# Dropping the step between load and first use where a tile was loaded ahead, and giving attention one more before its scores

## The chip, the cores and the metric

The kernel runs on one core of a Trainium2 chip, in one launch. The metric is device time in microseconds: the median of three runs. Names of engines: TensorE (PE in the profile, its weight loads PEld), VectorE (DVE), ScalarE (ACT), GpSimd (POOL), SyncE (SP, which issues the DMAs).

## The reference

One layer of an encoder, y = x + W_out @ concat[SSD, windowed attention, memory attention](RMSNorm(x)), in float32. It is applied to 1024 and to 256 tokens with shared weights: ten tiles of 128 tokens, with D_MODEL = 2048. Cut to what matters:

```python
proj = rms_norm(x, norm_g) @ w_in
xbc, z_ssd, dt_raw, q, k, v, z_att, mq, z_mem = split_cols(proj, IN_SIZES)
# SSD: conv + silu on xbc, a chunked scan forwards and backwards, gate, norm
o_ssd = rms_norm((y_f + y_b + d_skip * xs) * silu(z_ssd), ssd_norm_g)
# attention: 8 query heads and 2 key heads of 64, |t - s| <= 128, ALiBi, one sink logit a head
q, k = rms_norm(q, q_norm_g), rms_norm(k, k_norm_g)
o_att = window_attention(q, k, v, sink) * silu(z_att)
# memory attention: 4 heads of 128 over 256 memory rows
mk, mv = split_cols(rms_norm(mem, mem_norm_g) @ w_mem_kv, (MEM_WIDTH, MEM_WIDTH))
mq, mk = rms_norm(mq, mq_norm_g), rms_norm(mk, mk_norm_g)
o_mem = softmax(mq @ mk.T * 128 ** -0.5) @ mv * silu(z_mem)
y = x + concat([o_ssd, o_att, o_mem]) @ w_out
```

## The kernel before, in words

**The large products.** Rows of x (and later of the mixed outputs) stand on chip as a high and a low part (`xH`, `xL`, float32r); weights stream from DRAM in tiles `wraw` and are split into `wh` on ScalarE (L206) and `wl` on VectorE (L207). Each product is three matmuls: high by high, high by low, low by high. `block_tok` makes a block of 512 columns for five token tiles (L258 to L260, 15 matmuls of 128x512 for each of 16 steps k); `block_feat` makes 256 features by 640 tokens (L293 to L295); `block_pair` makes pairs of half blocks from sums of weights (L1268 to L1270). The rings: three or four buffers for `wraw`, four each for `wh` and `wl` (`RB`, `WB`), five PSUM banks `acc` for the blocks and three PSUM buffers `mix` (`psum(...)`) for everything else.

**The small work beside them.** Key preparation (`k_prep`), windowed attention (`attn`), memory attention (`mem_attn`) and the SSD scan (`dt_prep`, `ssd_up`, `ssd_down`) are Python generators, one for each tile of 128 tokens. They stand in two queues, `lanes`: lane 0 holds keys, attention and memory attention, lane 1 the SSD. While a block is built, `pump` resumes the generators so many times for each k as `RATES` says for that block (some 2 each for every k of `block_tok`, half of it for `block_feat`). What a generator issues from one `yield` to the next is a step. Steps thus set where its instructions stand among the block's. A scheduler then orders each engine's instructions by priority and by its estimate of when they can start, so neighbours in program order may change places; the weight splits have a raised priority. Each engine works through its list in order.

**Loading ahead.** `attn`, `mem_attn` and `k_prep` call `fetch_next` shortly before they end. It looks at the next entry of lane 0 and, if it is one of these three kinds, issues the DMA of its rows (`k_fetch`, `q_fetch`, `mq_fetch`, L485 to L498) into the pool `wa` of five buffers, and keeps the buffer in `fetched`. The next generator begins with `taken(...)`, which gives that buffer, or issues the load itself if there is none. Before the change every generator then yields once, loaded ahead or not, before the first instruction that reads the rows: a Square on ScalarE (L517 in `k_prep`, L632 in `attn`, L749 in `mem_attn`), or, in `mem_attn` for tiles 0 to 4, whose rows are stored the other way round, four transposes on TensorE (`pmq`, L744).

**Attention.** After the Square come the sums and the power on GpSimd, the scaling of q, and in two halves the split copies `qh`, four transposes into PSUM `pq` (L653) and the copy to `qT` (L655). One step later `scores(0)` begins: two matmuls a head into `psc` (L671, L672), a fused minimum on VectorE (L673), the exponential on ScalarE (L677), then transposes `ppt` (L693) with copies `pT` on ScalarE (L694), and the products with the values `po` (L703).

The order in which the work is queued in lane 0 is: `mem_values`, `k_prep` 0 to 4, `attn` 0 to 3, `mem_attn` 0 to 4, `k_prep` 5 to 9, `attn` 4, `attn` 5 to 9; later `mem_attn` 5 to 7, `mem_swap`, `mem_values`, `mem_attn` 8 and 9.

Of the kernel before, what the change touches and what calls it, by code (L numbers as in the profile page):

```python
# [44 lines left out]
def hymba_encoder_kernel(  # L45
# [37 lines left out]
    def psum(name):  # L83
        return mix.tile([P, 512], F32, tag="mix", name=name)
# [37 lines left out]
    def rsqrt(dst, src, scale, n):  # L122
        G.tensor_scalar(out=dst, in0=src, scalar1=scale, scalar2=EPS, op0=ALU.mult, op1=ALU.add)
        G.tensor_tensor(out=dst, in0=dst, in1=mhalf[:, :n], op=ALU.pow)

    def hv(ap, n=8):
        return ap.rearrange("p (h d) -> p h d", h=n)

    def hb(ap, n, d):
        return ap.unsqueeze(2).broadcast_to([P, n, d])  # L130
# [284 lines left out]
    def w2(name):  # L415
        return mp.tile([P, 512], F32, tag="wa", name=name, bufs=WA)
# [64 lines left out]
    fetched = {}  # L481
# [21 lines left out]
    def taken(name, t):  # L503
        return fetched.pop((name, t)) if (name, t) in fetched else fetch[name](t)

    def fetch_next():

        name = lanes[0][1][0] if len(lanes[0]) > 1 else ("", 0)
        if name[0] in fetch:
            fetched[name] = fetch[name[0]](name[1])  # L510

    def k_prep(t):
        r = taken("k_prep", t)
        yield
        ss = sm.tile([P, 2], F32, tag="s2", name="kss", bufs=4)
        sq = w2("ksq")[:, :P]
        A.activation(sq, r, AF.Square)  # L517
        V.reduce_sum(out=ss, in_=hv(sq, 2), axis=AX.X)
        rr = sm.tile([P, 2], F32, tag="s2", name="krr", bufs=4)
        rsqrt(rr, ss, 1.0 / 64, 2)  # L520
        yield
        r3 = hv(r, 2)
        V.tensor_mul(r3, r3, hb(rr, 2, 64))
        V.tensor_mul(r3, r3, gq.unsqueeze(1).broadcast_to([P, 2, 64]))

        kh = mp.tile([P, 4, 2, 64], F32R, tag="wa", name="kh", bufs=WA)
        for d in range(2):
            A.activation(kh[:, 0:2, d, :], r3, AF.Copy)
        for d in range(2):
            V.tensor_sub(kh[:, 2:4, d, :], r3, kh[:, 0:2, 0, :].bitcast(F32))  # L530
        yield
        yield
        ps = psum("pk")
        kf = kh.rearrange("p a b d -> p (a b d)")
        for a in range(4):
            T.transpose(ps[:, a * P:(a + 1) * P].bitcast(F32R), kf[:, a * P:(a + 1) * P], identr)
        sl = t if t < 5 else t - 3
        c = slice(sl * P, (sl + 1) * P)
        V.tensor_copy(kT[:, :, c], hv(ps[:, :256], 2))
        A.activation(kL[:, :, c], hv(ps[:, 256:], 2), AF.Copy)  # L540
        fetch_next()
        yield
# [77 lines left out]
    def attn(t):  # L620
# [5 lines left out]
        s0 = k0 if t < 4 else k0 - 3  # L626
        grp, ti = divmod(t, 5)
        tc_ = slice(ti * P, (ti + 1) * P)
        q = taken("attn", t)
        yield  # L630
        sq = w2("sq")
        A.activation(sq, q, AF.Square)  # L632
        ss = sm.tile([P, 8], F32, tag="s8", name="qss", bufs=4)
# [22 lines left out]
            qT.append(o)  # L656
        z = w2("za")
        S.dma_start(hv(z, 4), zT_d[0][grp][:, :, tc_])
        yield
        ns8 = nsink.rearrange("p (v r) -> p r v", v=2)  # L660
        state_ = {}
# [72 lines left out]
    def mem_attn(t):  # L734
        grp, ti = divmod(t, 5)
        tc_ = slice(ti * P, (ti + 1) * P)
        qr = taken("mem_attn", t)
        q = qr.bitcast(F32)
        yield

        def turned():
            ps = psum("pmq")
            for h in range(4):
                T.transpose(ps[:, h * P:(h + 1) * P].bitcast(F32R), qr[:, h * P:(h + 1) * P], identr)  # L744
            return ps

        tok_ = turned() if grp == 0 else q
        sq = w2("sq")
        A.activation(sq, tok_, AF.Square)  # L749
        ss = sm.tile([P, 4], F32, tag="s4", name="mss", bufs=4)  # L750
        V.reduce_sum(out=ss, in_=hv(sq, 4), axis=AX.X)
        r = sm.tile([P, 4], F32, tag="s4", name="mr", bufs=4)
        rsqrt(r, ss, 1.0 / P, 4)
        yield
        feat_ = q if grp == 0 else turned()
        qh = mp.tile([P, 512], F32R, tag="qT", name="mqh", bufs=2)
        A.activation(qh, feat_, AF.Copy)
        ql = mp.tile([P, 512], F32R, tag="qT", name="mql", bufs=2)
        V.tensor_sub(ql, feat_, qh.bitcast(F32))
        z = w2("zm")  # L760
        S.dma_start(hv(z, 4), zT_d[1][grp][:, :, tc_])
        yield
        yield
        st_ = {}

        def scores(hp):
            ps = psum("pms")
            for j in range(2):
                h = 2 * hp + j
                c = slice(h * P, (h + 1) * P)  # L770
                o = ps[:, j * 256:(j + 1) * 256]
                T.matmul(o, qh[:, c], mkH[:, h, :], start=True, stop=False)
                T.matmul(o, qh[:, c], mkL[:, h, :], start=False, stop=False)
                T.matmul(o, ql[:, c], mkH[:, h, :], start=False, stop=True)
            m = sm.tile([P, 2], F32, tag="m2", name="mm", bufs=10)
            V.reduce_max(out=m, in_=hv(ps, 2), axis=AX.X)
            V.scalar_tensor_tensor(out=m, in0=m, scalar=-1.0, in1=r[:, 2 * hp:2 * hp + 2], op0=ALU.mult, op1=ALU.mult)
            pr = mp.tile([P, 512], F32, tag="lg", name="mpr", bufs=2)
            den = sm.tile([P, 2], F32, tag="m2", name="mden", bufs=10)
            for j in range(2):  # L780
                A.activation(pr[:, j * 256:(j + 1) * 256], ps[:, j * 256:(j + 1) * 256], AF.Exp,
                             scale=r[:, 2 * hp + j:2 * hp + j + 1], bias=m[:, j:j + 1], accum_out=den[:, j:j + 1])
            V.reciprocal(out=den, in_=den)
            for j in range(2):
                c = slice(j * 256, (j + 1) * 256)
                V.tensor_scalar(out=pr[:, c], in0=pr[:, c], scalar1=den[:, j:j + 1], scalar2=0.5,
                                op0=ALU.mult, op1=ALU.mult)
            st_[hp] = pr

        def turn_(hp):  # L790
            pr = st_[hp]
            pt = psum("pmt")
            for a in range(4):
                T.transpose(pt[:, a * P:(a + 1) * P], pr[:, a * P:(a + 1) * P], ident)
            if hp == 0:
                st_["pT"] = mp.tile([P, 2, 768], F32, tag="pT", name="mpT", bufs=1)
            pT = st_["pT"][:, hp, :512]
            A.activation(pT, pt, AF.Copy)
            st_[hp] = pT

        oT = w2("moT")

        def values(hp):
            pT = st_.pop(hp)
            po = psum("pmo")
            for j in range(2):
                h = 2 * hp + j
                for a in range(2):
                    T.matmul(po[:, j * P:(j + 1) * P], mv[:, a, h * P:(h + 1) * P],
                             pT[:, (2 * j + a) * P:(2 * j + a + 1) * P], start=(a == 0), stop=(a == 1))  # L810
            c = slice(hp * 256, (hp + 1) * 256)
            V.tensor_mul(oT[:, c], po[:, :256], z[:, c])

        scores(0)
        yield
        scores(1)
        yield
        yield
        yield
        turn_(0)  # L820
        yield
        turn_(1)
        yield
        values(0)
        fetch_next()
        yield
        values(1)
        S.dma_start(oT_d[1][grp][:, :, tc_], hv(oT, 4))
        yield
# [653 lines left out]
    def refill_o(grp, when):  # L1483
        def f(k):
            if k not in when:
                return []
            q = when[k]
            need((attn, mem_attn, ssd_down, ssd_down)[q], range(grp * 5, grp * 5 + 5))
            return [part(fill_direct, q, j, oT_d[q][grp][:, j, :],
                         gain=None if q < 2 else vec[:, R_SG + 4 * (q - 2) + j:R_SG + 4 * (q - 2) + j + 1])  # L1490
                    for j in range(4)]
        return f
# [76 lines left out]
    for u, unit in enumerate(units):  # L1569
# [44 lines left out]
        extra=lambda k: some_left() if left else None)  # L1614
    queue(0, k_prep, range(5))
    queue(0, attn, range(4))
    queue(1, dt_prep, [0])

    def when_done(n, then):
# [9 lines left out]
        return f  # L1629

    queue(0, mem_attn, range(5))
    run(block_tok(w_in_rows("z1"), 5, ev_gate(1, 0)), RATES[0]["z1"], refill_x(1),
        extra=when_done(1, lambda: queue(1, ssd_up, range(4))))
# [25 lines left out]
    tok("mq", w_in_rows("mq"), ev_raw(mq_d, 5), grp=1)  # L1659
    gate("zm", 1, refill_o(0, {3: 0, 7: 1}))  # L1660
    queue(0, mem_attn, range(5, 8))
    queue(0, mem_swap, [0])
    queue(0, mem_values, [1])
# [97 lines left out]
```

## Time and profile before

| What | Value |
|---|---|
| median of three runs | 1785.77 us (1785.28 to 1787.44) |
| the profiled execution's own time | 1785.96 us |
| its span, first to last instruction | 1784.2 us |
| TensorE busy | 1774.6 us, 99% |
| VectorE, ScalarE, GpSimd busy | 1245.8, 921.5, 547.3 us |
| DMA queue of SyncE | 299.06 MB, 54.5% of 16 engines' span |
| granted TensorE clock | 1.000 |

How to read it: busy times are sums over one execution. A matmul's end is modelled, so a busy TensorE may hold some waiting. In the list of waits a row names the engine, tile and line that waited, behind the arrow what released it, then us in total, times and the longest. In a group's row stand busy us and mean ns, then the idle time just before its instructions and what ended it. A timeline row begins with start and duration in us, and in square brackets has the idle time before it and its releaser. In a row of the busy time by stage stand the stretch and its length, then busy us and number of instructions for PE, PEld, DVE, ACT and POOL, the granted clock, the DMA engines' share and GB/s. L numbers are lines of the kernel.

### The profile page before, as it was taken

Reading aid. Unit: us, or ns where it says so; the run is one execution under the profiler, and the core shown is the slowest. Engines: PE = TensorE matmul, PEld = TensorE weight load, DVE = VectorE, ACT = ScalarE, POOL = GpSimd, SP = SyncE. Lnnn points to the kernel's source line nnn. Section 1 sums busy time; section 2 is a strip of 40 time slices with the busy share of each in tenths; the row PEclk is TensorE's granted clock in tenths of the full one; section 3 lists DMA queues with packets and bytes.
Section 4 is the critical chain, followed back from the end, with each engine's and each line's share of the span. In section 5 each row is a group of like instructions: output and inputs, shape, how many; then the busy total and the mean of one; then the engine's idle time right before and its main releaser. Section 6 shows DMA issues by size and latency. Waiting matters only on the chain.

```text
span 1784.2 us, 31407 instructions
## 1 busy us (share of the span) xinstructions
PE 1774.6 (99%) x10838; PEld 1606.3 (90%) x10838; DVE 1245.8 (70%) x2358; ACT 921.5 (52%) x2049; POOL 547.3 (31%) x900
## 2 busy tenths in 40 slices
PE   9999999999999999999999999999999999999999
PEld 7889999999998999999889977877988888899999
DVE  5596788888768887777665666557777644766665
ACT  5555455555434766756464565544447533533333
POOL 0105789999810100001001010000100000057775
PEclk9999999999999999999999999999999999999999
DMA  8654454445446644453635645557777764744442
GB/s 299 191 183 125 135 154 148 141 146 159 126 144 205 199 134 139 135 162 110 189 118 175 193 148 160 168 158 249 229 229 242 247 189 140 224 147 142 148 142 78
DMA packets 208207, 301.12 MB, mean 169 GB/s; under 512 B 19568, under 2 KB 86192, under 8 KB 208048
## 3 DMA queue, kind: packets, MB, share of 16 engines
q1 hardware_dynamic: 207904, 299.06, 54.5%
q8 instruction: 85, 1.39, 0.3%
q14 instruction: 74, 0.61, 0.1%
q10 hardware_dynamic: 144, 0.06, 0.0%
HBM read 236.36 MB, written 62.69 MB: 168 GB/s over the span
## 4 chain that ended last, share of the span: by engine, by line
PE 82%; issue 6%; DVE 4%; DMA 4%; POOL 2%; ACT 1%; SPq 0%; POOLq 0%; ACTq 0%; DVEq 0%
PE acc L258 9%; PE acc L260 8%; PE acc L259 8%; PE acc L1268 7%; PE acc L1270 7%; PE acc L1269 7%; PE acc L293 5%; PE acc L295 5%; PE acc L294 5%; PE accm L1268 3%; PE accm L1269 3%; PE accm L1270 3%; PE po L703 1%; PE ppt L693 1%; PE py L970 1%
## 5 line engine op out<-in xcount | busy, mean ns | idle before, releaser
L207 DVE TENSOR_TENSOR wl<-wraw,wh 128x512 fp32r<-128x512 f32 (+1 forms) x480 | 346.2, 723 | 244.0 <-ACT wh L206 238.5
L206 ACT ACTIVATE wh<-wraw 128x512 fp32r<-128x512 f32 (+1 forms) x480 | 292.2, 613 | 312.4 <-PE acc L260 147.8
L258 PE MATMUL acc<-wh,xH 128*128 128x512 f32 (+1 forms) x1088 | 418.9, 385 | 0.4 <-DVE v_all L337 0.4
L260 PE MATMUL acc<-wh,xL 128*128 128x512 f32 (+1 forms) x1088 | 410.1, 377 | 0.0
L259 PE MATMUL acc<-wl,xH 128*128 128x512 f32 (+1 forms) x1088 | 409.7, 377 | 0.0
L258 PEld LDWEIGHTS acc<-wh,xH 128*128 128x128 f32 x1088 | 204.5, 188 | 37.8 <-issue 3.4
L260 PEld LDWEIGHTS acc<-wh,xL 128*128 128x128 f32 x1088 | 204.4, 188 | 37.0 <-issue 0.2
L259 PEld LDWEIGHTS acc<-wl,xH 128*128 128x128 f32 x1088 | 204.7, 188 | 35.9 <-issue 1.6
L293 PE MATMUL acc<-xH,wh 128*128 128x320 f32 x640 | 202.8, 317 | 0.0
L294 PE MATMUL acc<-xL,wh 128*128 128x320 f32 x640 | 198.8, 311 | 0.0
L295 PE MATMUL acc<-xH,wl 128*128 128x320 f32 x640 | 198.0, 309 | 0.0
L206 ACT ACTIVATE sh<-ws 128x384 fp32r<-128x384 f32 x176 | 91.3, 523 | 204.8 <-POOL ws L1236 102.5
L207 DVE TENSOR_TENSOR sl<-ws,sh 128x384 fp32r<-128x384 f32 x176 | 123.8, 706 | 94.6 <-ACT sh L206 94.4
L1236 POOL TENSOR_TENSOR ws<-wraw 128x128 f32<-128x128 f32 x176 | 110.8, 630 | 205.8 <-DMA wraw<-in_w_in_pairs_dram 80.9
L665 POOL COPY lg<-nsink 128x2 f32<-128x2 f32 x40 | 13.6, 340 | 379.1 <-PE ppt L693 221.3
L1236 POOL TENSOR_TENSOR ws<-wraw,ws 128x128 f32<-128x128 f32 x176 | 118.7, 674 | 13.8
L293 PEld LDWEIGHTS acc<-xH,wh 128*128 128x128 f32 x640 | 120.2, 188 | 2.8 <-issue 2.2
L294 PEld LDWEIGHTS acc<-xL,wh 128*128 128x128 f32 x640 | 120.3, 188 | 1.7 <-issue 1.4
L295 PEld LDWEIGHTS acc<-xH,wl 128*128 128x128 f32 x640 | 120.2, 188 | 0.6 <-issue 0.5
L1236 POOL TENSOR_TENSOR wraw<-wraw 128x128 f32<-128x128 f32 x176 | 112.9, 642 | 13.7
L1236 POOL TENSOR_TENSOR ws<-ws,wraw 128x128 f32<-128x128 f32 x176 | 115.6, 657 | 0.0
L362 DVE SCALAR_TENSOR_TENSOR c<-u,vec,c 128x638 f32<-128x638 f32 (+1 forms) x96 | 90.0, 938 | 9.9 <-ACT c L357 9.5
(437 smaller groups left out, 3942.7 us busy)
## 6 DMA issues: line engine op xcount, KB each, us to landing
wraw<-in_w_in_laid_dram SPq DMA_DIRECT2D x176, 256.0 KB, 3.0
wraw<-in_w_in_pairs_dram SPq DMA_DIRECT2D x112, 256.0 KB, 2.7
wraw<-in_w_out_laid_dram SPq DMA_DIRECT2D x64, 256.0 KB, 3.5
wraw<-in_w_out_pairs_dram SPq DMA_DIRECT2D x64, 256.0 KB, 2.8
rf<-ac SPq DMA_DIRECT2D x40, 256.0 KB, 4.1
rb<-ac SPq DMA_DIRECT2D x40, 256.0 KB, 4.7
wraw<-in_w_mem_laid_dram SPq DMA_DIRECT2D x32, 256.0 KB, 4.4
xst<-in_x_sample_dram SPq DMA_DIRECT2D x20, 256.0 KB, 5.9
```

What stands on the lines that cost most here:

```text
L206: a = A.activation(h, raw, AF.Copy)
L207: b = V.tensor_sub(l, raw, h.bitcast(F32))
L258: T.matmul(ps[t][:, :n], sh, h[:, :n], start=(k_ == 0), stop=False)
L259: T.matmul(ps[t][:, :n], sh, l[:, :n], start=False, stop=False)
L260: T.matmul(ps[t][:, :n], sl, h[:, :n], start=False, stop=(k_ == KT - 1))
L293: T.matmul(o, sh, cur["H", q][:, m, c], start=(k == 0), stop=False)
L294: T.matmul(o, sh, cur["L", q][:, m, c], start=False, stop=False)
L295: T.matmul(o, sl, cur["H", q][:, m, c], start=False, stop=(k == KT - 1))
L1236: G.tensor_tensor(out=o, in0=x, in1=y, op=op)
L1268: T.matmul(ps[p], h, xh, start=(k_ == 0), stop=False)
L1269: T.matmul(ps[p], h, xl, start=False, stop=False)
L1270: T.matmul(ps[p], l, xh, start=False, stop=(k_ == 7))
```

## The change

In the three generators the `yield` behind `taken(...)` is left out when the rows were loaded ahead (`early_`); otherwise it stays. In `attn` a second `yield` stands between the turn of the queries (with the load of the gate `z`) and `scores(0)`. No operation, DMA, buffer or rate is changed.

```diff
     def k_prep(t):
+        early_ = ("k_prep", t) in fetched
         r = taken("k_prep", t)
-        yield
+        if not early_:
+            yield
...
     def attn(t):
...
+        early_ = ("attn", t) in fetched
         q = taken("attn", t)
-        yield
+        if not early_:
+            yield
         sq = w2("sq")
         A.activation(sq, q, AF.Square)
...
         z = w2("za")
         S.dma_start(hv(z, 4), zT_d[0][grp][:, :, tc_])
+        yield
         yield
...
     def mem_attn(t):
...
+        early_ = ("mem_attn", t) in fetched
         qr = taken("mem_attn", t)
         q = qr.bitcast(F32)
-        yield
+        if not early_:
+            yield
```

How it moves instructions is seen in the order of each engine. First TensorE, where attention of tile 0 goes from the turn of its second half of queries (`pq`) to its first scores (`psc`); `acc` rows are the block's matmuls. Before:

```order
L295 MATMUL acc<-xH_6806,wl 128x320
L653 MATMUL pq<-identr,qh 128x128 x4
L671 MATMUL psc<-kT,qT 128x256
L672 MATMUL psc<-kL,qT 128x256
L293 MATMUL acc<-xH_6938,wh 128x320
```

The same place of the changed kernel (`py` are products of the SSD, from lane 1):

```order
L295 MATMUL acc<-xH_7454,wl 128x320
L657 MATMUL pq<-identr,qh 128x128 x8
L977 MATMUL py<-rb,xs 64x128 x16
L676 MATMUL psc<-kT,qT 128x256
L677 MATMUL psc<-kL,qT 128x256
L676 MATMUL psc<-kT,qT 128x256
```

The scores stood right behind the transposes and now have sixteen products of the SSD ahead of them; the two halves' transposes stand together, and so do the first scores.

Second ScalarE, at the first use of the rows of attention tile 9 (`sq<-q`), which tile 8 has loaded ahead; `pT` are the copies of tile 8's turned probabilities, `so` and `zq` or `zd` belong to `ssd_down`. Before:

```order
L206 ACTIVATE wh<-wraw 128x512
L694 ACTIVATE pT<-ppt 128x256 x4
L632 ACTIVATE sq<-q 128x512
L1040 ACTIVATE so<-pr 128x512
L1098 ACTIVATE zq,yss<-yd 128x512
```

The same place of the changed kernel:

```order
L699 ACTIVATE pT<-ppt 128x256 x2
L636 ACTIVATE sq<-q 128x512
L206 ACTIVATE wh<-wraw 128x512
L1105 ACTIVATE zd,yss<-yd 128x512
L699 ACTIVATE pT<-ppt 128x256 x2
L1047 ACTIVATE so<-pr 128x512 x2
```

The Square has moved ahead of the last two copies of the probabilities, and so has a load to wait for ahead of them; behind it still stand the copies `so` out of PSUM.

## The prediction

> **What bounds the kernel now.** I read the page first, then TensorE's waits and the busy time by stage for the stretch from 530 to 1470 us, where the edited generators run; then what ScalarE waits for, the landings, and single places on the timeline.
>
> ```profile
> span 1784.2 us, 31407 instructions
> PE 1774.6 (99%) x10838; PEld 1606.3 (90%) x10838; DVE 1245.8 (70%) x2358; ACT 921.5 (52%) x2049; POOL 547.3 (31%) x900
> PEclk9999999999999999999999999999999999999999
> ```
>
> TensorE is busy for 99% of the span at the full granted clock. Its work is the same in both kernels: the diff moves steps and adds no operation. So the time can change only by what TensorE waits. The busy time by stage shows how much that is where the change acts:
>
> ```profile
> 530.00:600.00 70.00, 69.67 (x354) 59.24 (x353) 62.39 (x129) 39.20 (x93) 6.54 (x10) 1.00 0.68 207
> 600.00:930.00 330.00, 328.21 (x2239) 301.59 (x2239) 245.69 (x555) 200.69 (x502) 26.68 (x40) 1.00 0.48 144
> 930.00:1240.00 310.00, 309.94 (x1778) 258.80 (x1778) 190.55 (x433) 172.04 (x432) 28.16 (x56) 1.00 0.56 176
> 1240.00:1470.00 230.00, 228.73 (x1350) 195.92 (x1349) 153.57 (x304) 117.62 (x279) 15.63 (x30) 1.00 0.73 229
> sum 940.00, PE 936.55 PEld 815.55 DVE 652.20 ACT 529.55 POOL 77.01; mean PE 234.14 PEld 203.89 DVE 163.05 ACT 132.39 POOL 19.25
> ```
>
> The first figure after each stretch's length is TensorE's busy time. Over 940 us it idles 940 - 936.55 = 3.45 us. That is about all a better order can give back: 0.19% of the time. Matmul ends are modelled, so a little waiting may hide inside busy time. The named waits of that stretch are:
>
> ```profile
> PE pmt L794 <- DVE mpr L786: 1.4, 2, 1.3
> PE pyb L1091 <- ACT so L1040: 0.6, 1, 0.6
> PE pd L1074 <- DVE nm L673: 0.5, 1, 0.5
> PE pk L536 <- DVE kh L530: 0.3, 1, 0.3
> PE psc L671 <- ACT pT L694: 0.2, 1, 0.2
> PE psc L671 <- ACT qT L655: 0.2, 1, 0.2
> ```
>
> Total us, times, longest: they add to 3.2 us. The wait that the added step addresses (scores at L671 on the turned queries qT) is the last, 0.2 us.
>
> **The change part by part.** First the counts. A tile is "loaded ahead" when the task before it in lane 0 has called `fetch_next` for it. By the `queue` calls these are `k_prep` 1 to 9 (tile 0 follows `mem_values`, which fetches nothing), all ten `attn`, and `mem_attn` 0 to 4, 6, 7 and 9: 27 tiles. `k_prep` and `mem_attn` lose 9 + 8 = 17 steps of lane 0; `attn` loses one and gets one back.
>
> *The added step* puts more of the block's matmuls between the copy of qT and the first scores. What waits there now, TensorE's row and its weight loads' row from the groups of that stretch, with one case from the timeline:
>
> ```profile
> L671 PE MATMUL psc<-kT,qT 128*128 128x384 f32 (+1 forms) x80 | 27.9, 354 | 0.5 <-ACT pT L694 0.2 <-ACT qT L655 0.2
> L671 PEld LDWEIGHTS psc<-kT,qT 128*128 128x128 f32 x80 | 15.0, 188 | 5.9 <-ACT pT L694 2.2 <-ACT qT L655 1.3 <-DVE nm L673 0.7
> 677.35 0.46 PE L653 MATMUL pq<-identr,qh 128*128 128x128 f32 x4
> 678.86 0.44 PE L671 MATMUL psc<-kT,qT 128*128 128x384 f32 x1 [0.19 <-ACT qT L655]
> ```
>
> The gain lies between 0.2 us (matmul row) and 1.3 us (all idle of the weight loads that qT ended). I take the middle, 0.8 us. The step costs no instruction; lane 0 gets it back from the dropped one.
>
> *The dropped step, on ScalarE.* The first use of a loaded tile is a Square on ScalarE (L517, L632, L749), which takes its instructions in order: whatever stands behind waits with it. Two uses in following attention tiles give the length of a step:
>
> ```profile
> 1041.23 0.63 ACT L632 ACTIVATE sq<-q 128x512 f32<-128x512 f32 x1
> 1088.91 0.63 ACT L632 ACTIVATE sq<-q 128x512 f32<-128x512 f32 x1
> ```
>
> An attention tile is 21 steps, so a step of lane 0 is (1088.91 - 1041.23) / 21 = 2.3 us. The waits of these three lines on their loads, and the landings (KB, median us):
>
> ```profile
> ACT ksq L517 <- DMA kr<-k: 7.2, 4, 3.7
> ACT sq L632 <- DMA q<-q: 3.9, 2, 2.2
> ACT sq L749 <- DMA mq<-mq: 3.6, 2, 2.3
> q<-q SPq DMA_DIRECT2D x10, 256.0 KB, 3.1
> mq<-mT SPq DMA_DIRECT2D x5, 256.0 KB, 3.3
> mq<-mq SPq DMA_DIRECT2D x5, 256.0 KB, 4.6
> kr<-k SPq DMA_DIRECT2D x10, 64.0 KB, 3.2
> ```
>
> So already now 8 uses wait, 7.2 + 3.9 + 3.6 = 14.7 us together: the dropped step was cover that did not always suffice. What such a wait costs TensorE is seen once:
>
> ```profile
> 1237.62 0.42 SPq L490 DMA_DIRECT2D q<-q  x1
> 1241.23 0.63 ACT L632 ACTIVATE sq<-q 128x512 f32<-128x512 f32 x1 [2.19 <-DMA q<-q]
> 1241.77 0.58 ACT L1040 ACTIVATE so<-pr 128x512 f32<-128x512 f32 x1
> 1242.40 1.12 PE L1091 MATMUL pyb<-state,cc 128*128 128x512 f32 x2 [0.59 <-ACT so L1040]
> ```
>
> ScalarE stood 2.19 us for the load of attention tile 9; behind it stood the copy `so` that empties a bank of the three-buffer PSUM pool; TensorE waited 0.59 us for that bank. The other waits have no TensorE row behind them. So the price is 0.6 us in 14.7, or 4%, on average, and 0.59 / 2.19 = 27% where it hits.
>
> The added wait has a floor of 0 and a ceiling of 27 x 2.3 = 62 us. The floor is real: in the order shown with the change the Square has moved past one pair of copies only, because instructions are ordered by estimated readiness and not simply by step. At 4% that is 0 to 2.5 us on TensorE, and 27% of 62 is the far end, 16.8 us. I take half of 2.5: 1.2 us.
>
> The load row for `kr` gives 3.2 us for 64 KB and that for `q` 3.1 us for 256 KB. [...]
>
> *The dropped step, on TensorE.* In `mem_attn` 0 to 4 the first use is not ScalarE's but the transposes `pmq` (L744), so TensorE itself meets the load. The tightest case:
>
> ```profile
> 833.68 0.52 SPq L496 DMA_DIRECT2D mq<-mT  x1
> 839.86 0.45 PE L744 MATMUL pmq<-identr,mq 128*128 128x128 f32 x4
> ```
>
> From issue to transposes are 6.2 us; less 3.3 us of landing and 2.3 us for the step, 0.6 us is left. So a place like it just holds, and one that moves by two steps waits 1.7 us. With five such tiles the cost is between 0 and 5 x 1.7 = 8.5 us; one wait of half that size, 0.8 us, is nearest to the row.
>
> *SyncE and VectorE.* No load, and no store, is added; the loads ahead are issued at the same step as now, only the uses come sooner. Behind a Square that waits stand weight splits too, but their wh and wl rings hold four tiles, so the blocks' matmuls have cover of several us. The other waits of the list (pmt, pd, pk) depend on how the two lanes fall together; lane 0 runs up to 17 steps early against lane 1, so each may go or come. I count them as zero and give them to the range.
>
> **Sum.** -0.8 + 1.2 + 0.8 = +1.2 us on the span: 1785.4 us. The profiled run's own time is 1785.96 us, 1.8 us above its span, and 0.2 us above the median of the three runs, 1785.77. On that median the forecast is 1785.77 + 1.2 = **1787.0 us**.
>
> **The rivals.** *Slower: loads hold the in-order queues.* The same mechanism at its higher price. For: eight uses wait now, with only one step less to come. Against: seven of the eight cost TensorE nothing visible, and ScalarE is only 52% busy. If the price on TensorE is 15% (midway between 4% and 27%) of 62 us, that is 9.3 us, less 0.8: 1794.3 us; at the far end 16.8 + 8.5 - 0.8 = 24.5 us, 1810 us, which would need every use to wait a full step. It decides from about 4.4 us of new waits on (7% of 62 us, or two or three late `pmq`), where the total passes 0.2%.
>
> *Faster: the waits in the stretch go.* If qT, the PSUM bank and the pmt wait of 1.3 us all fall away and none comes, the time drops by 3.45 us to 1782.3 us. For: lane 0 is displaced against lane 1 almost everywhere. Against: it has to remove everything and add nothing, and 1782.3 us is just short of 0.2%: to pass it, waiting hidden in busy time must go too.
>
> *It does nothing that counts.* The ordering by readiness undoes the shorter step, TensorE's queue hides the rest: 1785.8 us. This is inside the forecast's case.
>
> **How the numbers follow.** About 0.2% (3.6 us) is what a measurement of this kernel can tell from no change. Forecast and nothing together: 0.55. Slower: 0.32, since the waits are real, one has reached TensorE, and the room upward is five times that downward. Faster: 0.13, since 3.45 us is nearly the whole room. The likeliest case alone holds 1783 to 1789.3 us. For 8 in 10 the range goes down to 1783.0 us, leaving 0.09 of the faster case, and up to 1793.5 us, leaving about 0.1 of the slower one.
>
> **What would show it.** Right: TensorE's busy time within 2 us of 1774.6; the qT wait at the scores gone; `ksq` and `sq` waiting on loads for 15 to 40 us in all; idle in the stages still 3 to 6 us. Wrong: a `pmq` or scores row with a releaser "DMA", or TensorE's idle over 8 us between 530 and 1470 us (slower), or under 1 us (faster); or a changed sum of TensorE's work, which I hold to be impossible.

## The result: slower, 1796.4 us

The changed kernel took 1796.42 us (median of 5 runs, 1795.27 to 1799.52), the kernel before 1786.15 us in 5 runs beside it (1785.28 to 1787.44). The ratio is 1.0058, 95% interval 1.0045 to 1.0071. Ratios and intervals are formed from all runs of a comparison and can differ by some 0.06% from the quotient of the two medians. The forecast was 1787.0 us, its range ended at 1793.5. The profiled execution of after took 1795.27 us, 1.7 us above its span.

**The profile after.** The head of the page, then the busy time by stage with the same stretches as before:

```profile
span 1793.6 us, 31405 instructions
PE 1778.0 (99%) x10838; PEld 1607.8 (90%) x10838; DVE 1245.9 (69%) x2358; ACT 922.6 (51%) x2049; POOL 544.1 (30%) x900
...
530.00:600.00 70.00, 69.15 (x354) 58.93 (x353) 63.89 (x135) 42.08 (x102) 8.43 (x12) 1.00 0.67 213
600.00:930.00 330.00, 324.65 (x2218) 298.57 (x2217) 241.84 (x549) 196.66 (x493) 24.65 (x40) 0.99 0.46 139
930.00:1240.00 310.00, 308.80 (x1767) 256.75 (x1766) 192.09 (x429) 170.76 (x428) 27.72 (x54) 1.00 0.54 169
1240.00:1470.00 230.00, 227.56 (x1340) 194.78 (x1339) 149.97 (x298) 119.67 (x282) 16.52 (x30) 1.00 0.74 233
sum 940.00, PE 930.16 PEld 809.02 DVE 647.79 ACT 529.17 POOL 77.32; mean PE 232.54 PEld 202.26 DVE 161.95 ACT 132.29 POOL 19.33
```

TensorE has the same 10838 matmuls. It idles 940 - 930.16 = 9.84 us in the stretch where it idled 3.45, so 6.4 of the 9.4 us by which the span grew are idle time there. Its busy time grew as well, by 3.4 us, and the granted clock of one stage is 0.99. TensorE's waits over the whole run:

```profile
PE psc L676 <- ACT qT L659: 2.4, 1, 2.4
PE pd L1081 <- DMA ydT<-yd: 1.5, 1, 1.5
PE pmt L801 <- DVE mpr L793: 1.3, 1, 1.3
...
PE pk L538 <- DVE kh L532: 0.8, 1, 0.8
PE ppt L698 <- ACT pT L699: 0.8, 1, 0.8
PE pmq L751 <- DMA mq<-mT: 0.8, 1, 0.8
```

They are single events at different places. The largest is at the very scores before which the change puts a step. The timeline of attention tile 1 shows why (start, duration, engine, line; idle time before it and releaser in brackets):

```profile
666.39 0.33 SPq L888 DMA_DIRECT2D rf<-ac  x1
...
667.41 0.59 ACT L659 ACTIVATE qT<-pq 128x512 fp32r<-128x512 f32 x1
...
669.75 0.46 PE L657 MATMUL pq<-identr,qh 128*128 128x128 f32 x4
...
670.66 0.99 ACT L960 ACTIVATE rf<-rf,wj_all 128x128 f32<-128x128 f32 x3 [1.74 <-DMA rf<-ac]
...
672.89 0.57 ACT L659 ACTIVATE qT<-pq 128x512 fp32r<-128x512 f32 x1
...
673.51 0.44 PE L676 MATMUL psc<-kT,qT 128*128 128x384 f32 x1 [2.44 <-ACT qT L659]
```

The turned queries were complete in `pq` by about 670.2 us. Ahead of their copy to `qT`, on ScalarE, stood the additions of the other lane, which wait for that lane's own load `rf` (SSD, L888, not one of the rows fetched ahead). The load was issued at 666.39 us and landed 4.2 us later. ScalarE stood 1.74 us for it, did its four parts and two more instructions, and only then copied `qT`; TensorE waited 2.44 us. In before the same additions, the seventh group of `rf` in both kernels, stand ahead of both copies of this tile:

```profile
665.23 0.33 SPq L881 DMA_DIRECT2D rf<-ac  x1
...
668.37 1.28 ACT L953 ACTIVATE rf<-rf,wj_all 128x128 f32<-128x128 f32 x4
...
674.06 0.58 ACT L655 ACTIVATE qT<-pq 128x512 fp32r<-128x512 f32 x1
```

They began when their load had landed, and the first copy came 5.7 us later. The second copy, at 678.23 us, has the next group ahead of it, which began at 674.53 us and waited for no load; TensorE waits 0.19 us there. In after the load is issued 1.2 us later than in before, and the two copies stand 6.7 and 5.3 us earlier, so the group has come between them: attention moved against the other lane. From 674.89 us on the clock is halved. The busy time by stage, cut at that point:

```profile
671.50:674.89 3.39, 1.38 (x9) 1.38 (x10) 1.88 (x6) 3.39 (x10) 0.00 (x0) 1.00 0.57 171
674.89:678.30 3.41, 3.41 (x15) 3.41 (x15) 2.73 (x9) 0.75 (x4) 0.00 (x0) 0.50 0.21 68
```

The granted clock was 0.50 for 3.41 us, which is half of 3.41, about 1.7 us of matmul time lost: in this execution the wait of 2.4 us cost about 4.1. With the 6.4 us of idle time 8.1 of the 9.4 us are named; 1.3 us, in busy time or outside the stretch, are not assigned. The half clock doesn't set the time of after: two of the five executions have a mean clock of 1.000, without such a stretch, and took 1795.72 and 1796.42 us.

The waits of the fetched rows did grow, as the prediction had it:

```profile
ACT sq L636 <- DMA q<-q: 11.8, 5, 3.3
...
ACT sq L756 <- DMA mq<-mq: 5.4, 2, 4.3
...
ACT ksq L519 <- DMA kr<-k: 2.7, 3, 1.3
```

They sum to 19.9 us on ScalarE where before had 14.7. A fourth line reads fetched rows on ScalarE, the copy `mqh` of memory attention 0 to 4 (L757, now L764), which the prediction leaves out: it waited for them 3.4 us in before and 10.4 us in after. One of these waits reached TensorE, at attention tile 6:

```profile
1072.53 0.63 ACT L636 ACTIVATE sq<-q 128x512 f32<-128x512 f32 x1 [1.28 <-DMA q<-q]
...
1073.88 1.61 ACT L699 ACTIVATE pT<-ppt 128x384 f32<-128x384 f32 x4
...
1074.40 0.55 PE L698 MATMUL ppt<-identr,lg 128*128 128x128 f32 x3 [0.83 <-ACT pT L699]
```

Behind the Square that stood 1.28 us for its rows stood the copies `pT` of the tile before, and TensorE waited 0.83 us for the first of them. With the 0.8 us of `pmq` the fetched rows cost TensorE 1.6 us here, where before had 0.59.

### The profile page after: what moved, and what is told of

It is laid out like the page before. It is cut to its first block, busy times and chain, and to the rows that moved or that the text cites. A ratio compares the mean times of both kernels' runs of the same rounds, so it can differ in the third digit from the quotient of the medians.

```text
span 1793.6 us, 31405 instructions
## 1 busy us (share of the span) xinstructions
PE 1778.0 (99%) x10838; PEld 1607.8 (90%) x10838; DVE 1245.9 (69%) x2358; ACT 922.6 (51%) x2049; POOL 544.1 (30%) x900
## 4 chain that ended last, share of the span: by engine, by line
PE 81%; issue 6%; DVE 5%; DMA 4%; ACT 2%; POOL 1%; SPq 0%; DVEq 0%; ACTq 0%; POOLq 0%
PE acc L258 9%; PE acc L260 9%; PE acc L259 9%; PE acc L1277 7%; PE acc L1275 7%; PE acc L1276 7%; PE acc L293 5%; PE acc L295 5%; PE acc L294 4%; PE accm L1276 3%; PE accm L1275 3%; PE accm L1277 3%; PE po L708 1%; PE ppt L698 1%; DVE wl L207 1%
## 5 line engine op out<-in xcount | busy, mean ns | idle before, releaser
L1243 POOL TENSOR_TENSOR ws<-wraw 128x128 f32<-128x128 f32 x176 | 115.0, 653 | 209.3 <-DMA wraw<-in_w_in_pairs_dram 80.5
L1243 POOL TENSOR_TENSOR ws<-wraw,ws 128x128 f32<-128x128 f32 x176 | 114.8, 652 | 13.8
```

Of the source, the lines that this page charges most:

```text
L1243: G.tensor_tensor(out=o, in0=x, in1=y, op=op)
```

## The experiments

Two theories stood against each other. **A, displacement:** by the dropped steps lane 0 runs earlier against the blocks' matmuls and lane 1, and waits arise at places that have nothing to do with the fetched rows. Tiles of `k_prep` 1 to 4 lose a step each, so attention 0 to 3 start four steps earlier (some four k of the blocks there, hence "block steps" below). By the count of dropped steps attention 4 to 9 are 14 steps early; attention 9 begins its Square at 1211.3 us where before has 1241.2. Memory attention 5 stands with the blocks again: its Square is at 1321.6 us, in before at 1314.4. **B, cover:** the rows are used too soon after their load, and what stands behind them waits. The kernels of one comparison ran on one chip with their own runs of before; ratios, not times, are compared across them.

### Displacement alone, cover alone, drop alone, addition alone

Displacement alone keeps the step before first use and drops a later, empty one of the same tile, in `k_prep` and `mem_attn`; attention as before:

```diff
-        yield                      # k_prep: ahead of pk; mem_attn: ahead of turn_(0)
+        if not early_:
+            yield
```

> Lane 0 is displaced as by the change (17 steps fewer in key preparation and memory attention), but the step between load and first use stays everywhere; a later step is dropped instead, and attention is as before. Theory A (the two lanes meet at other places, and the time is lost where they collide): about the changed kernel's time, 1793 to 1798 us, and a long TensorE wait near 673 us with the half clock behind it. Theory B (the loads come too late for their first use): as before, 1785 to 1788 us.

Measured: 1796.09 against 1787.46 us, ratio 1.0046 (1.0031 to 1.0061). The loss is nearly whole with every row's step kept; the three lines wait 15.1 us for their rows, where before has 14.7, and `mqh` 10.8. The long wait expected near 673 us did not come; the longest is 1.7 us, for `cb` of the other lane, and ends at 726.1 us. Two parts of this trace are not displacement. The transposes `pk` waited 1.6 us at 597.68 us, where the dropped step had stood between `kh` and them. And near 150 us, ahead of every edited tile, TensorE waited 0.8 us more than in before, and then its matmuls of 128x320 took 0.47 us each instead of 0.31 up to 156.9 us, at half the clock: some 2.5 us together.

Cover alone makes the whole change, but `k_prep` and `mem_attn` give the step back later in the same tile:

```diff
-        yield                      # between load and first use
+        if not early_:
+            yield
...
+        if early_:
+            yield                  # given back after the first use
```

> All of the change, but key preparation and memory attention give the dropped step back later in the same tile, so lane 0 keeps its place against lane 1 from tile to tile and only the cover of the loads is gone. Theory A: near the time before, 1785 to 1789 us, with ScalarE's waits for the three loads grown to 20 us or more all the same. Theory B: 1793 us or more.

Measured: 1788.37 against 1787.46 us, ratio 1.0002 (0.9992 to 1.0011). The same 27 tiles use their rows a step sooner, and nothing is lost. Its ScalarE waits on the fetched rows, and the sum of the stages:

```profile
ACT ksq L519 <- DMA kr<-k: 5.6, 3, 3.3
...
ACT sq L638 <- DMA q<-q: 4.5, 4, 2.3
...
ACT sq L758 <- DMA mq<-mq: 1.4, 1, 1.4
...
sum 940.00, PE 934.81 PEld 814.66 DVE 653.70 ACT 528.71 POOL 76.02; mean PE 233.70 PEld 203.67 DVE 163.42 ACT 132.18 POOL 19.00
```

11.5 us of waits, less than before's 14.7 and not the 20 that A expected, with a step less of cover; TensorE idles 5.2 us. All of the change without its displacement costs nothing, and displacement without less cover costs most of it: the dropped cover is not the cause. What 20 us of waits would cost in the order of before is not tested, since they did not arise.

The dropped step without the added one (27 steps fewer):

> The step is dropped in all three generators; attention gets none back, so lane 0 loses 27 steps instead of 17. Theory A: another place of the lanes, 1788 to 1800 us, not ordered by the number of steps. Theory B: at least the changed kernel's time, 1796 us or more, since the same loads are late.

Measured: 1789.62 against 1787.46 us, ratio 1.0011 (1.0002 to 1.0020), far from B's 1796. Lane 0 is displaced further here than in after (each attention tile adds one more), yet most of the loss is gone. So displacement isn't costly by its size. At the place of the long wait the same load makes ScalarE stand almost as long:

```profile
665.20 0.33 SPq L887 DMA_DIRECT2D rf<-ac  x1
...
666.65 0.60 ACT L659 ACTIVATE qT<-pq 128x512 fp32r<-128x512 f32 x1
...
669.38 0.99 ACT L959 ACTIVATE rf<-rf,wj_all 128x128 f32<-128x128 f32 x3 [1.49 <-DMA rf<-ac]
...
669.52 0.34 PE L675 MATMUL psc<-kT,qT 128*128 128x384 f32 x1
```

Both copies of `qT` had been made before ScalarE met the load, so TensorE did not wait for it.

The added step alone (ten steps more):

> Only the added step in attention; every load keeps its cover, and lane 0 becomes 10 steps longer. Theory A: displaced the other way, anything from 1785 to 1797 us. Theory B: 1785 to 1787 us, the wait for the turned queries at most 0.2 us less.

Measured: ratio 0.9998 (0.9988 to 1.0007): nothing.

### The parts of the change

Each part is that generator's own hunk of the change.

> The change in key preparation alone: 9 steps of lane 0 fewer, so attention 0 to 3 starts four steps early against the SSD, as in the changed kernel; memory attention and later tiles are displaced by half as much as there. Theory A (place of the lanes): the waits between 600 and 700 us come back, 1789 to 1794 us. Theory B (late loads): 9 of 27 loads late, at most a third of the loss, 1788 to 1790 us.

Keys alone: 1793.13 against 1787.18 us, ratio 1.0027 (1.0018 to 1.0037), in A's range and above B's. Its longest wait, 2.0 us for `cb`, ends at 724.4 us, not between 600 and 700.

> The change in memory attention alone: nothing moves before memory attention 0 (about 800 us); later tiles by one to six steps of a block. Theory A: no wait near 673 us, 1785 to 1790 us. Theory B: TensorE meets the loads at the transposes of the first five tiles, 1788 to 1791 us with rows of a load as releaser there.

Memory attention alone: 1790.96 against 1787.18 us, ratio 1.0018 (1.0008 to 1.0027). This is above A's range and in B's, and one wait of TensorE on a load is there, 0.5 us at `pmq`. The run cuts cover and displaces at once, so it does not tell the two apart.

> The change in attention alone: the step between load and first use goes and comes back before the scores, so no tile of lane 0 is displaced. Theory A: the time before, 1785 to 1788 us. Theory B: ten loads late, of those the longest waits, 1788 to 1791 us.

Attention alone, which cuts the cover of ten loads and displaces nothing: 0.9988 (0.9979 to 0.9998). This would have been a version that beats both kernels, so it ran again, with more runs:

> The change in attention alone once more, in five rounds: the step between load and first use goes in attention's fetched tiles, and the step between the turn of the queries and the scores comes. It displaces nothing and cuts the cover of ten loads. Theory A: 1785 to 1787 us, ratio 0.998 to 1.000, as in its first run. Theory B: 1787.5 or more. It is also the version that may beat both kernels.

Measured: 1.0007 (0.9997 to 1.0016). The two intervals hardly touch. Together they say no difference, and that an interval of +-0.1% from one comparison is a little too narrow to trust. No version is shown to beat the kernel before. The two traces of this one kernel idle 6.3 and 4.9 us between 530 and 1470 us, so a difference of 1.4 us in the idle time of single traces says little.

### Repairing the place

After with four empty steps ahead of the first attention tile, so that attention 0 to 3 stand where they stood:

```diff
+        for _ in range(4 if t == 0 else 0):
+            yield
```

> All of the change, with four empty steps ahead of attention 0, so that attention 0 to 3 stands where it stood before against the SSD; the later tiles stay displaced as in the changed kernel, by somewhat less. Theory A: the wait near 673 us and the half clock behind it go, and 3 to 6 us with them: 1789 to 1793 us. Theory B: no difference from the changed kernel, 1796 us.

Measured: 1797.51 against 1787.18 us, ratio 1.0059 (1.0043 to 1.0075): A missed, and the time is the one that B expected. But the three lines' waits on fetched rows are 15.8 us, near the 14.7 of before. The wait at 673 us went, and others came:

```profile
PE pq L659 <- ACT qT L661: 2.5, 1, 2.5
PE pr L1047 <- DVE oT L713: 1.9, 1, 1.9
PE ppt L700 <- ACT pT L701: 1.6, 2, 1.3
```

The first is in attention tile 2, which stands where it stood: ahead of its copy `qT` on ScalarE stood a copy `fh` of the other lane, which waited 3.8 us for that lane's load `rb`. The others lie in later tiles; those from the second key tiles to attention 9 remain 5 to 10 steps early. So the one wait that the trace of after shows best does not explain the loss as a whole.

### Displacement without any edit of the change

One of three empty steps in the preparation of the four memory key tiles (`mk_prep`), which lane 0 does ahead of the keys, is taken out. The three generators of the change are those of before.

```diff
         yield
         yield
-        yield
         ps = psum("pmk")
```

> The kernel before, with one of the three empty steps in the preparation that precedes lane 0's key tiles taken out. The three generators of the change are untouched, every tile keeps its step between load and first use, and attention has no added step; but every lane 0 tile from the first key tile on stands four block steps earlier (attn 0 to 3 by 4, later tiles by 2 to 4). Theory A (what costs is where lane 0 stands against the blocks and the other lane): the loss comes again without any edit of the change, as with the change in the keys alone, which displaces attn 0 to 3 alike: 1789 to 1794 us, TensorE idle 6 to 9 us between 530 and 1470. Theory B (late loads): nothing is late, 1786 to 1788 us, idle 3 to 4.

Measured: 1792.64 against 1786.49 us, ratio 1.0037 (1.0026 to 1.0047). Its waits on the fetched rows are in sum about those of before (6.9 + 4.3 + 3.9 = 15.1 us), and TensorE idles 940 - 932.68 = 7.3 us, with the longest waits again at places of their own. First TensorE's waits, then what stands behind the largest on the timeline, then the sum of the stages:

```profile
PE pyb L1090 <- DVE oT L705: 2.5, 1, 2.5
PE psc L670 <- ACT cb L858: 1.4, 1, 1.4
...
PE pmk L448 <- DVE mkr L443: 1.2, 1, 1.2
...
1242.62 0.63 ACT L631 ACTIVATE sq<-q 128x512 f32<-128x512 f32 x1 [3.22 <-DMA q<-q]
...
1246.31 0.69 DVE L640 TENSOR_TENSOR q<-q,qr 128x512 f32<-128x512 f32 x1 [0.85 <-POOL qr L636]
...
1246.92 0.42 DVE L705 TENSOR_TENSOR oT<-po,za 128x256 f32<-128x256 f32 x1
...
1247.39 1.71 PE L1090 MATMUL pyb<-state,cc 128*128 128x512 f32 x2 [2.50 <-DVE oT L705]
...
sum 940.00, PE 932.68 PEld 810.64 DVE 649.08 ACT 528.05 POOL 77.14; mean PE 233.17 PEld 202.66 DVE 162.27 ACT 132.01 POOL 19.28
```

Four steps of displacement, with every step of cover kept, cost 0.37%. Of this the 1.2 us at `pmk` (0.07%) is no displacement: there the dropped step had stood. And the longest wait hangs on a row fetched ahead. ScalarE stood 3.22 us for attention 9's rows; VectorE, which needs that Square for the scaling of the queries, did the scaling ahead of the product `oT` of the tile before, and TensorE waited 2.50 us for `oT`. In before the same load cost 0.59 us. The repair's 1.9 us wait for `oT` has the same order, behind a wait of 1.55 us for attention 9's rows. So B's mechanism is at work in single places, though no step of cover is gone in this run: where lane 0 stands decides what waits behind a load.

The other direction, four empty steps ahead of the first attention tile of before:

> The kernel before with four empty steps ahead of the first attention tile: attn 0 to 3 stand four block steps later, the later tiles 2 to 5. Every load has its step and more. Theory A in the strict form (the order before was a fit, any displacement loses): 1789 to 1794 us. Theory A in the loose form (only some places collide): 1785 to 1794, as the waits fall. Theory B: 1786 to 1788, since loads are only earlier against their use.

Measured: 0.9997 (0.9988 to 1.0006): nothing. The strict form of A falls; the loose form and B both allow this.

Is it lane against lane, or lane 0 against the blocks? The keys alone, with lane 1 moved four steps forward too (`ssd_up(0)` waits 2 steps instead of 6):

> The change in the key tiles alone, and lane 1's first ssd_up tile waits 2 steps instead of 6, so that lane 1 moves four steps earlier with lane 0 between 600 and 740 us: the lanes' place against each other is that of before for attn 0 to 3, their place against the blocks is not. If the place of lane against lane decides, the wait near 724 us of the keys alone goes and the time is under 1789.5 us; if the place against the blocks decides, waits of 1 us and more stay between 600 and 740 us and the time is 1791 to 1795.

Measured: 1794.34 us, ratio 1.0040 (1.0027 to 1.0053). By its time this speaks for the blocks. By its waits it does not: the long wait near 724 us went, and the stage that holds attention 0 to 3 is as busy as in before (328.58 against 328.21 us). The loss stands ahead of and behind it:

```profile
530.00:600.00 70.00, 67.80 (x336) 56.27 (x335) 63.77 (x139) 42.87 (x105) 7.51 (x10) 1.00 0.68 209
600.00:930.00 330.00, 328.58 (x2248) 302.15 (x2247) 245.97 (x556) 197.42 (x489) 26.50 (x40) 1.00 0.46 141
...
1240.00:1470.00 230.00, 226.39 (x1332) 194.89 (x1331) 148.80 (x293) 116.58 (x273) 14.39 (x29) 0.99 0.73 232
```

TensorE's busy time is 1.9 us less than in before up to 600 us, where the shortened key tiles wait at `pk` (0.6 and 1.2 us), and 2.3 us less from 1240 us on, where it stood 2.22 us for the load `ydT` at 1302.6. This points to lane against lane for the waits between 600 and 740 us of the keys alone, and to new waits made by moving lane 1 as well. Some 2.6 us of this trace's loss lie near 150 us, as in displacement alone, ahead of every moved tile. One run doesn't settle it.

The size of the displacement was scanned with two more points later, one more earlier, and one run that returns the four early steps at attention 0, so that only the key tiles stand early:

> As the run with lane 0 four steps earlier, but the empty step is taken out of two of the four memory key tiles only: lane 0 stands two steps earlier from the first key tile on. If the loss grows smoothly with earliness, half of 0.37%: 1788 to 1790.5 us. If it hangs on single places, anything from 1784 to 1795, and not between the values at 0 and -4 except by chance.

> The kernel before with two empty steps ahead of the first attention tile. If only earlier displacement costs: 1785 to 1788 us. If single places decide: as likely 1789 or more.

> The kernel before with eight empty steps ahead of the first attention tile. If only earlier displacement costs: 1785 to 1788 us. If single places decide: as likely 1789 or more; a displacement twice as large gives no larger loss than the four steps by itself.

> Lane 0 four steps earlier from the first key tile on, and four empty steps ahead of the first attention tile, so that attention 0 to 3 stand where they stand in the kernel before. If the loss of 0.37% comes from attention 0 to 3 standing early: back to 1786 to 1788.5 us. If it comes from the key tiles before them: 1791 to 1794 us.

| Attention 0 to 3 displaced by | Median and that of before, us | Ratio | 95% interval |
|---|---|---|---|
| -4 | 1792.64, 1786.49 | 1.0037 | 1.0026 to 1.0047 |
| -2 | 1793.89, 1788.61 | 1.0035 | 1.0022 to 1.0047 |
| 0, key tiles 4 early | 1791.71, 1788.61 | 1.0019 | 1.0007 to 1.0031 |
| +2 | 1789.60, 1788.61 | 1.0009 | 0.9999 to 1.0018 |
| +4 | 1786.71, 1786.49 | 0.9997 | 0.9988 to 1.0006 |
| +8 | 1792.35, 1788.61 | 1.0023 | 1.0013 to 1.0032 |

There is no smooth dependence: -2 costs as much as -4, +8 costs and +4 does not. None of the six gains. The +8 run is the cleanest case of displacement: it only adds steps, so no wait of it is that of a dropped step, and it loses 0.23%. Returning the steps at attention 0 takes the loss from 0.37% to 0.19%, with intervals that overlap a little, which is neither of the two outcomes expected. The rest contains the wait at `pmk`, 0.9 us in its trace, so it is not shown that the key tiles themselves cost. In the comparison of the four later points the runs of before spread more (1785.42 to 1795.04 us), and the profiled executions of -2 (1789.66 us), +8 (1790.05) and the run with the steps returned (1789.01) were the shortest of their kernels, so the traces were not used for the cause of their loss.

## Why the prediction was wrong, step by step

- *TensorE bounds the kernel, and only its waits can change.* Right, but for one thing: its work is the same, its busy time is not. I held a changed sum to be impossible; it rose by 3.4 us, of which about 1.7 is the half clock. Two of the signs named for "slower" came: a `pmq` row with the releaser DMA, and 9.84 us of idle time between 530 and 1470 us.
- *The added step, -0.8 us.* The qT wait did not go; it is 2.4 us instead of 0.2. The term looked at the distance between copy and scores. What decided was what ScalarE had to do ahead of the copy. With the added step by itself no wait of the scores on qT is listed, and it is worth nothing that can be measured (0.9998).
- *The dropped step on ScalarE, +1.2 us.* The waits became 19.9 us, inside the 15 to 40 named, so 5.2 us were added. The term stands for half of 62 us, and 14.7 + 31 would be 46 us, more than the range names. The average price held: 0.83 us of 19.9 is again 4%. The price where it hits, 27%, was 65% here (0.83 of 1.28 us) and 78% in the run four steps early (2.50 of 3.22 us). Cutting the same cover without displacement cost 0.02% (-0.08% to +0.11%).
- *The dropped step on TensorE, +0.8 us.* It came as sized, once, in memory attention; the queued load was issued 4 us before:

```profile
878.39 0.52 SPq L496 DMA_DIRECT2D mq<-mT  x1
...
882.34 0.51 PE L751 MATMUL pmq<-identr,mq 128*128 128x128 f32 x4 [0.76 <-DMA mq<-mT]
```

- *"The other waits of the list (pmt, pd, pk) depend on how the two lanes fall together ... I count them as zero and give them to the range."* This is the step that failed. It noted that lane 0 would run up to 17 steps early (14 at a time, by the count above) and priced that at nothing, with gain and loss alike. In before TensorE idles 3.45 us of 940, so another order of the same work had little to gain and more to lose. The runs showed displacement by itself to cost up to 0.46%: 0.35% to 0.46% in the three that move lane 0 early as a whole (6.3 to 8.2 us, with the other parts named there), 0.23% at +8 and nothing measurable at +4. With 8 us more in the sum the forecast would have been 1795; but nothing known beforehand gave that size, and an honest term was a range from 0 to some 8 us.
- *The slower rival.* "Loads hold the in-order queues" gave 1794.3 us, near the result, and that is luck: it took 15% of 62 us of added waits on the fetched rows, and 5.2 us were added. Its mechanism is half right. ScalarE's queue, worked in order, did hold TensorE up; in the longest wait of after, 2.44 us, the load that held it belonged to the other lane, in which the diff changes nothing, and fetched rows cost TensorE 1.6 us. But the dropped step was not what made these waits costly: with it dropped and nothing displaced the time was that of before.

Not settled: which places make up the loss of after. The repair of one moved it to others, and a larger displacement (drop alone) costs only 0.11%. Whether a displacement loses could not be told from its size or sign. How much of each loss comes from loads (fetched or of the other lane) that hold a queue, and how much from other waits, was not measured apart.

## What to carry to other kernels

Where the bounding engine idles 0.2% and its order has grown around interleaved work, an edit that takes steps out of a generator is first of all a displacement of everything after it; price that, before the local gain, and test it by displacing alone, with the edited code left as it is. To judge a local edit, give the steps back in the same tile, so that nothing after it moves. In the longest waits here a copy or product that TensorE needed stood on its engine behind an instruction of another task that waited for a load (`rf` in after, where TensorE waited 2.44 us; `rb` in the repair, 2.5 us; attention 9's rows in the run four steps early, 2.50 us). So look at what stands ahead of it, and at whose load.

## What the hardware showed beside it

Short waits of TensorE were followed by half the granted clock, in some traces and not in others. In four rows of busy time cut at that point the clock is 0.50 for 3.41 us: after (from 674.89 us, behind a wait of 2.44 us), displacement alone (727.09, behind 1.7), +4 (687.36, behind 2.12) and the repair (1233.08, behind 1.9). Three more starts lie in stages with a lower mean clock: keys alone (725.28, behind 2.0; 0.98 between 700 and 800 us), -4 (1247.80, behind 2.50) and keys with lane 1 moved (1304.04, behind 2.22), both 0.99 between 1240 and 1470 us. One stretch of 3.41 us at 0.50 would give 0.983 and 0.993 there. Near 150 us displacement alone (from 153.65 us) and keys with lane 1 moved (from 153.75) have matmuls of 128x320 of 0.47 us instead of 0.31, behind two waits of 0.83 and 0.82 and of 0.90 and 0.81 us; the mean clock of these two executions is 0.998, that of after, with one stretch, 0.999. In before's profiled execution the clock of 0.50 came only after the last instruction, at 1785.68 us. Other executions of before seem to have it too: 22 of the 105 run beside the experiments show a mean clock below 1.000, 21 of them 0.999, which fits one such stretch, and one 0.998; these took 2.4 to 3.0 us longer on average than the others of their comparison.

The length of a wait alone does not tell whether the half clock follows. In the repair, two waits, of 2.5 and 1.9 us: 3.41 us that hold most of each, then what came behind:

```profile
721.07:724.48 3.41, 1.73 (x12) 0.90 (x9) 2.07 (x9) 0.91 (x2) 0.00 (x0) 1.00 0.35 134
1229.67:1233.08 3.41, 1.55 (x11) 1.12 (x11) 3.02 (x6) 0.60 (x1) 0.28 (x2) 1.00 0.21 43
...
725.30:728.70 3.40, 3.40 (x25) 3.40 (x26) 2.62 (x5) 1.23 (x2) 0.00 (x0) 1.00 0.23 77
1233.08:1236.49 3.41, 3.41 (x10) 2.67 (x9) 2.80 (x5) 0.72 (x2) 0.00 (x0) 0.50 0.88 263
```

The longer wait ended at 725.25 us, and the clock is 1.00 before and behind it. The shorter one left TensorE busy for 1.55 us of 3.41, and the clock behind it is 0.50. Cover alone has a wait of 1.8 us (`pst` for `fh`) and a mean clock of 1.000, displacement alone the half clock behind 1.7 us. What decides was not shown. Nor need the half clock show in the time of a kernel: the profiled execution of the +4 run had one such stretch, and its ten runs lost nothing (0.9997).
